# A two-layer streaming trunk: the first modulation entry by halves out of PSUM, and one gate vector worked out in the first FFN instead of the mixer

## The chip, the cores and the metric

The kernel runs on one core of a Trainium2 chip. The metric is the device time of one execution in microseconds (us). The time before is the median of three runs, 1248.64 us (1246.87 to 1248.95). All numbers below come from these runs and from one execution that the hardware profiler recorded.

## The reference

The model has two layers over 512 frames of width 1024, in fp32: one with an HGRN2 mixer and a SwiGLU FFN, then a K/V projection that reads its result, then one with band attention over that K/V and a second FFN. Every norm is followed by a shift and a scale, and every sublayer is added to the residual through a gate; shifts, scales and gates are rows of one product of silu(c) with `mod_w`. Cut to what matters here:

```python
c_act = jax.nn.silu(c)
for layer in range(2):
    mod = c_act @ mod_w[layer] + mod_b[layer]          # 1024 x 6144
    sh1, sc1, g1, sh2, sc2, g2 = jnp.split(mod, 6, axis=-1)
    u = modulate(rms_norm(h, norm_mix[layer]), sh1, sc1)   # u * (1 + scale) + shift
    mix = hgrn2_mixer(u, ...) if layer == 0 else chunk_band_attention(u, k, v, ...)
    h = h + g1[:, None, :] * mix
    u = modulate(rms_norm(h, norm_ffn[layer]), sh2, sc2)
    gate, up = jnp.split(u @ ffn_w_in[layer], 2, axis=-1)
    h = h + g2[:, None, :] * ((jax.nn.silu(gate) * up) @ ffn_w_out[layer])
    if layer == 0:
        k, v = shared_kv(h, c_act, ...)                # its own shift and scale
return rms_norm(h, final_norm)

# at the end of hgrn2_mixer, per head:
o = o * lax.rsqrt(jnp.mean(o * o, axis=-1, keepdims=True) + eps) * o_gain
o = o * silu(g)
return o.reshape(...) @ w_out
```

## The kernel before

**Layout.** Activations lie transposed: 8 blocks of 128 channels on the partitions, 512 frames along the free axis. A matrix product in fp32 is made as three passes of rounded parts, high x high, low x high, high x low (`mm3`, L184 to L186 in the profile). ScalarE makes each high part (names with `_h`; L120, L517), VectorE each low part (`_l`; L127, L518). The second and larger part of each FFN's input runs as "fast" tiles with seven products in place of eight: their weights `w1` to `w4` are combined on VectorE from the loaded blocks `c1` and `c2` (`f_x`, L531 to L536), then split, and their matmuls carry L552 to L554. The first FFN's tile 0 is made during the norm, tiles 1 to 3 are plain, and the rest are fast.

**Modulation vectors.** A vector has eight entries of 128 channels, one column each. For an entry a row of `mod_w` transposed, 128 x 1024, is loaded from HBM, and VectorE multiplies it with `crow`, silu(c) copied to all partitions, and sums along the free axis into one column (L334). The names are `mw{i}_{j}`: vector i, entry j; 4 is `sh2`, 5 is `g2`, 13 is `sck`. A generator, `mod_vectors`, called `side`, makes one entry at each `next(side)`. It loads two entries ahead, on SyncE's queue, into four buffers. `state["mods_after"]` names the instruction behind which a scheduler may put such an entry. In the mixer `side` is drawn from between pieces of filler work (`push`), and in the last head pair at the steps that `LAST` lists. `drain(side)` ahead of the stage `ao` (the mixer's output product) draws what is left. In the first FFN the next `side` is drawn from between fast tiles.

**The start.** Everything up to the first projections is in program order (`manual_schedule`). TensorE makes silu(c) on all partitions into two PSUM banks (`pcs`, tiles `crow0` and `crow1`). `KEEP` fill-up matmuls follow on TensorE (L978). ScalarE copies three quarters to `crow`, VectorE one quarter (L979 to L981). Then `mod_entry(0, 1)` makes the scale of the first block: product L634, column `a` on ScalarE (L637). `rounded` makes the high part of the first block (L656), `rest` the low part (L659), `high` and `low` those of the first weights (`first_h` L644, `first_l` L647), and the first matmuls follow (L683). The loads of rows, of `h` and of the first weights alternate on SyncE's queue.

**End of the mixer.** The last head pair runs `core(3)`: product `o`, squares summed on ScalarE (`osq`, L849), their scaling on VectorE (`oms`, L852), the power on GpSimd (`ors`, L854), the product with `o` on VectorE (`oe`, L860), transposes on TensorE (`ot`, L869), the gate (`yq`, L889), and the stage `ao`. What the scheduler has put ahead of an instruction on its engine's queue runs first. The rest of the order is chosen at build time by that scheduler, and is the same in every run.

Of the kernel before, what the change touches and what calls it, by code (L numbers as in the profile page):

```python
# [9 lines left out]
F32 = mybir.dt.float32  # L10
F32R = mybir.dt.float32r
U8 = mybir.dt.uint8
AF = mybir.ActivationFunctionType
ALU = mybir.AluOpType

P = 128
D = 1024
S = 512
KT = D // P
# [15 lines left out]
C_NM = C_KVB + 16  # L35
# [17 lines left out]
V1_AFTER, CREDIT, RATES = 1, 3.0, (3.5, 16, 2.0, 56, 1.5)  # L53


KEEP = 5


EARLY = (3, 5)
# [6 lines left out]
def trunk(ctx: ExitStack, tc: tile.TileContext, d, out):  # L66
    nc = tc.nc
    T, A, V, G = nc.tensor, nc.scalar, nc.vector, nc.gpsimd
# [3 lines left out]
    sm = ctx.enter_context(tc.tile_pool(name="sm", bufs=3))  # L72
# [6 lines left out]
    cols = cst.tile([P, NCOL], F32, tag="cols", name="cols")  # L79
# [56 lines left out]
    state = {"loaded": 0, "split": 0, "used": 0}  # L136
# [262 lines left out]
    def ffn(layer, z0, u, g2, side, finish):  # L399
        nm = f"f{layer}"  # L400
        fast = layer in FAST
        with tc.tile_pool(name=nm, bufs=1) as fp:
            a = []
            raw_a = {}
            FIRST = FT - 16
            if fast:
                his, los, sums = fast_inputs(fp, *u, nm)

                def slot(j, s):
                    return his[j][:, s, :], los[j][s // 2][:, s % 2, :]  # L410

                u = [(his[k // 2][:, 2 * (k % 2):2 * (k % 2) + 2, :].rearrange("p a c -> p (a c)"),
                      los[k // 2][k % 2].rearrange("p a c -> p (a c)")) for k in range(KT)]

            def activated(n):

                if not fast or n == FT - 1:
                    return sm.tile([P, S], F32, tag="sq", name=f"{nm}_at{n}", bufs=2)

                g, e = divmod(n, 2) if n < FIRST else divmod(n - FIRST, 4)  # L420
                if e == 0:
                    tag, m = (f"ab{g}", 2) if n < FIRST else (f"xs{g}", 4)
                    raw_a[n] = fp.tile([P, m, S], F32, tag=tag, name=f"{nm}_ar{n}")
                return raw_a[n - e][:, e, :]

            def kept(n, at):
                a.append(at if fast else usplit(fp, f"a{n}", at, f"{nm}_a{n}"))

            for n in range(PLAIN if fast else FT):
                sg = sm.tile([P, S], F32, tag="ut", name=f"{nm}_s{n}", bufs=2)  # L430
                at = activated(n)
                if n == 0:
                    (tg, bg), (tu, bu) = z0
                    A.activation(sg, tg, AF.Silu, bias=bg)
                    V.scalar_tensor_tensor(at, tu, bu, sg, op0=ALU.add, op1=ALU.mult)
                else:
                    res = []
                    drain(proj((nm, n, 0), u, res))
                    if not fast:
                        next(side, None)  # L440
                        next(side, None)
                    elif n in (2, 3):
                        sums(1, n == 3)
                    drain(proj((nm, n, 1), u, res))
                    if not fast:
                        next(side, None)
                    A.activation(sg, res[0], AF.Silu)
                    V.tensor_mul(at, res[1], sg)
                kept(n, at)
                if fast and n in (1, 2):  # L450
                    sums(0, n == 2)
            if fast:
                fast_tiles(fp, nm, slot, activated, kept, side)


            room = [("sp0", 1), ("sp1", 1)] + [(f"uo{j}", 2) for j in range(4)] + [("x1", 1), ("x2", 1)]
            room += [(f"ab{g}", 1) for g in range(FIRST // 2)] + [(f"xs{g}", 2) for g in range(4)]
            places = []

            def parts(k):  # L460
                if isinstance(a[k], tuple):
                    return a[k]
                if not places:
                    tag, m = room.pop(0)
                    t = fp.tile([P, 2 * m, S], F32R, tag=tag, name=f"{nm}_p{k}")
                    places.extend((t[:, 2 * i, :], t[:, 2 * i + 1, :]) for i in range(m))
                ah, al = places.pop(0)
                A.activation(ah, a[k], AF.Copy)
                V.tensor_sub(al, a[k], ah)  # L469
                a[k] = ah, al  # L470
                return a[k]

            chunks = ((0, 8), (8, 8), (16, 6))
            if fast:

                pss = [bank(f"{nm}_o{n}_0") for n in range(2)]
                for ci, (k0, nk) in enumerate(chunks):
                    ws = [weight((nm, "o", n, ci)) for n in range(2)]
                    for kt in range(nk):
                        k = k0 + kt  # L480
                        if k + 1 < FT:
                            parts(k), parts(k + 1)
                        for w, ps in zip(ws, pss):
                            mm3(ps, w, kt, a[k], k == 0, k == FT - 1)
                    for _ in range(2):
                        next(side, None)
                for n, ps in enumerate(pss):
                    residual(n, ps, g2)
                    later = finish(n, slice(0, S))
            for n in range(2 if fast else 0, KT):  # L490
                ws = []
                cuts = (slice(0, S),) if n < KT - 1 or not layer else (slice(0, CUT), slice(CUT, S))
                for c in cuts:
                    ps = bank(f"{nm}_o{n}_{c.start}")
                    for ci, (k0, nk) in enumerate(chunks):
                        if c.start == 0:
                            ws.append(weight((nm, "o", n, ci)))
                        for kt in range(nk):
                            k = k0 + kt
                            if c.start and k in later:  # L500
                                later.pop(k)()
                            mm3(ps[:, c], ws[ci], kt, [x[:, c] for x in a[k]], k == 0, k == FT - 1)
                        for _ in range(1 + (fast and ci == 0)):
                            next(side, None)
                    residual(n, ps, g2, c)
                    later = finish(n, c)
            drain(side)
# [96 lines left out]
    crow = mp.tile([P, D], F32, tag="crow", name="crow", bufs=1)  # L604
    mix = ctx.enter_context(ExitStack())
    hp = mix.enter_context(tc.tile_pool(name="hgrn", bufs=1))
# [5 lines left out]
    fraw, mrow, wfs, u, sqs, a1 = {}, {}, {}, {}, {}, []  # L612
# [18 lines left out]
    def mod_entry(j, v):  # L631
        raw = sm.tile([P, 1], F32, tag=f"m{v}", name=f"m{v}_{j}", bufs=4)
        mw = mrow.pop((j, v))
        V.scalar_tensor_tensor(mw, mw, 1.0, crow, op0=ALU.mult, op1=ALU.mult, accum_out=raw)  # L634
        r = sm.tile([P, 1], F32, tag=f"a{v}", name=f"a{v}_{j}", bufs=KT)
        if v:
            A.activation(r, raw, AF.Identity, scale=cols[:, C_NM + j:C_NM + j + 1], bias=gb[:, j:j + 1])  # L637
        else:
            A.activation(r, raw, AF.Identity, bias=cols[:, C_MB + j:C_MB + j + 1])
        return r  # L640

    def high(j):
        wfs[j] = [wp.tile([P, 6, P], F32R, tag="w" + x, name=f"first{j}_{x}") for x in "hl"]
        A.activation(wfs[j][0], fraw[j], AF.Copy)  # L644
# [41 lines left out]
    mod = {v: cst.tile([P, KT], F32, tag=f"mod_{v}", name=f"mod_{v}") for v in vectors[2:]}  # L686
# [251 lines left out]
            yield from output_gate(hd)  # L938

    late = []  # L940
    side = mod_vectors(("g1", "sc2", "sh2", "g2"), hp)
    MODS_FROM = 84
    fill = filler()
    pos = 0
# [13 lines left out]
    with tc.manual_schedule():  # L958
        dcs = hp.tile([P, KT, P], F32, tag="on3", name="dc")

        pcs = []
# [13 lines left out]
        gb = cst.tile([P, KT], F32, tag="gb", name="gb")  # L975
        V.scalar_tensor_tensor(gb, cols[:, C_MB + 8:C_MB + 16], 1.0, cols[:, C_NM:C_NM + KT], op0=ALU.add, op1=ALU.mult)
        for _ in range(KEEP):
            T.matmul(first[0][:, 0:256], ones, dcs[:, 0:2, :].rearrange("p k c -> p (k c)"), start=True, stop=True)  # L978
        A.activation(crow[:, 0:S], pcs[0], AF.Copy)  # L979
        A.activation(crow[:, S:S + 256], pcs[1][:, 0:256], AF.Copy)  # L980
        V.tensor_copy(crow[:, S + 256:D], pcs[1][:, 256:S])  # L981
        high(0)
        a1.append(mod_entry(0, 1))
        rounded(0)
        square(0)
        for j in range(KT):
# [98 lines left out]
        u = [u[j] for j in range(KT)]  # L1085
# [8 lines left out]
    on = [ons[i // 2][:, i % 2, :] for i in range(AH)]  # L1094
    ad = hp.tile([P, 2, NB, P], F32, tag="ad", name="ad")
    G.memset(ad, 0.0)
    LAST = {8: 3, 9: 1, 11: 1}
    for p in range(4):
        start, end = pos, ends[p]
        for i, _ in enumerate(core(p, *gate[p])):  # L1100
# [23 lines left out]
    for n in range(KT):  # L1124
# [4 lines left out]
        else:  # L1129
            res = []  # L1130
# [5 lines left out]
    z0, rb = early_pair((("f0", 0, 0), ("f0", 0, 1)), us, acc, "n1")  # L1136
# [3 lines left out]
    if 0 in FAST:  # L1140
        u = rb, a_f, mod["sh2"]
# [12 lines left out]

    shifts[("k", 0)] = shifts[("k", 1)] = mod["shk"]
    with tc.tile_pool(name="mx", bufs=1) as mx:
        ffn(0, z0, u, mod["g2"], mod_vectors(("sck", "shk", "sc1b", "sh1b", "g1b"), mx), finish)


    a_q = gain_scale(C_NM + KT, mod["sc1b"], "a_q")  # L1160
# [2 lines left out]
    with tc.tile_pool(name="attn", bufs=1) as ap:  # L1163
# [169 lines left out]
        for n in range(KT):  # L1333
# [4 lines left out]
            else:  # L1338
                res = []
# [215 lines left out]
```

## Time and profile before

| what | before |
|---|---|
| median of the runs | 1248.64 us (1246.87 to 1248.95) |
| the profiled execution | 1251.22 us |
| its span, first to last instruction | 1249.3 us |
| TensorE busy | 1230.0 us, 98% of the span |
| VectorE busy | 991.8 us, 79% |
| ScalarE busy | 648.1 us, 52% |
| GpSimd busy | 21.4 us, 2% |
| read from HBM | 171.96 MB |
| products of modulation rows, L334 | 96 in 115.6 us, 1219 ns each |

How to read the rows that follow. In the order of time a row is: start in us, length in us, engine, line, operation, output from inputs, shape and count, and in brackets the idle time ahead of it with the engine that ended it. In the chain of work that ended last a row is: start, length, what. In a view by stretches a row is: the stretch, busy us of the engines in the order TensorE, its weight loads, VectorE, ScalarE, GpSimd (with the count of instructions), the granted clock of TensorE as a share of full speed, the busy share of the DMA engines and GB/s; a row for TensorE alone leaves the other engines out. In a view of loads, "us from issue to landing" stands below the group's row.

### The profile page before, as it was taken

What the parts mean: (1) busy time and instruction counts of PE and PEld (TensorE: products, weight loads), DVE (VectorE), ACT (ScalarE), POOL (GpSimd) and SP (SyncE); (2) the same over time, 40 slices, a digit from 0 to 9 for tenths busy, and PEclk for the clock granted to TensorE, in tenths of its full rate; (3) what the DMA queues carried; (4) which work ended last, traced back from release to release, by engine and by line L of the source; (5) the groups of instructions that cost most, each with busy time, mean ns of one, the idle gap of its engine ahead of it and who ended that gap; (6) DMA issues with size and microseconds to landing.
All of it is one profiled execution on the core that took longest, in us unless ns stands there. A gap on an engine that the chain in (4) does not pass through costs nothing.

```text
span 1249.3 us, 21601 instructions
## 1 busy us (share of the span) xinstructions
PE 1230.0 (98%) x8548; PEld 1067.5 (85%) x8548; DVE 991.8 (79%) x1800; ACT 648.1 (52%) x1157; POOL 21.4 (2%) x29
## 2 busy tenths in 40 slices
PE   8999999999999999999999999999999999999997
PEld 7887778778899999988888877777889999998887
DVE  8986868877989999987668878996798999984323
ACT  6455446433655565642228556675455555573221
POOL 0100000000000000000000000000000000000000
PEclk9999999999999999999999999999999999999999
DMA  9632444543424444467752445531243444342331
GB/s 364 239 130 86 136 153 155 194 159 118 107 96 137 150 142 146 139 205 274 240 177 77 135 134 163 163 109 65 71 122 113 138 136 135 102 127 93 93 93 68
DMA packets 52533, 177.55 MB, mean 142 GB/s; under 512 B 5968, under 2 KB 8400, under 8 KB 52432
## 3 DMA queue, kind: packets, MB, share of 16 engines
q1 hardware_dynamic: 51856, 174.08, 42.4%
q0 software_dynamic: 576, 2.10, 1.0%
q8 instruction: 67, 1.10, 0.4%
q14 instruction: 34, 0.28, 0.1%
HBM read 171.96 MB, written 2.10 MB: 139 GB/s over the span
## 4 chain that ended last, share of the span: by engine, by line
PE 87%; DVE 6%; ACT 3%; issue 1%; DMA 1%; POOL 0%; DVEq 0%; POOLq 0%; ACTq 0%
PE f_r L553 10%; PE f_r L554 9%; PE f_r L552 9%; PE f_o L185 6%; PE f_o L186 6%; PE f_o L184 6%; PE f L184 2%; PE f L185 2%; PE f L186 2%; PE bo L1258 1%; PE bo L184 1%; PE ao L184 1%; PE ao L185 1%; PE ao L186 1%; PE bo L186 1%
## 5 line engine op out<-in xcount | busy, mean ns | idle before, releaser
L553 PE MATMUL f_r<-f_l,f_w_h 128*128 128x256 f32 x1008 | 287.8, 285 | 0.0
L554 PE MATMUL f_r<-f_h,f_w_l 128*128 128x256 f32 x1008 | 282.2, 280 | 0.0
L552 PE MATMUL f_r<-f_h,f_w_h 128*128 128x256 f32 x1008 | 281.2, 279 | 0.0
L552 PEld LDWEIGHTS f_r<-f_h,f_w_h 128*128 128x128 f32 x1008 | 190.1, 189 | 0.1
L553 PEld LDWEIGHTS f_r<-f_l,f_w_h 128*128 128x128 f32 x1008 | 190.0, 189 | 0.1
L554 PEld LDWEIGHTS f_r<-f_h,f_w_l 128*128 128x128 f32 x1008 | 189.3, 188 | 0.0
L185 PE MATMUL f_o<-f_p,f_o_h 128*128 128x512 f32 (+1 forms) x374 | 141.9, 379 | 0.1
L184 PE MATMUL f_o<-f_p,f_o_h 128*128 128x512 f32 (+1 forms) x374 | 141.8, 380 | 0.0
L186 PE MATMUL f_o<-f_p,f_o_l 128*128 128x512 f32 (+1 forms) x374 | 141.4, 379 | 0.0
L334 DVE SCALAR_TENSOR_TENSOR mw<-mw,crow 128x1024 f32<-128x1024 f32 x96 | 115.6, 1219 | 2.3 <-DMA mw<-in_modw 2.3
L120 ACT ACTIVATE f_o_h<-r_f_o 128x1024 fp32r<-128x1024 f32 (+1 forms) x48 | 46.8, 987 | 133.5 <-PE f_o L185 102.6
L127 DVE TENSOR_TENSOR f_o_l<-r_f_o,f_o_h 128x1024 fp32r<-128x1024 f32 (+1 forms) x48 | 54.1, 1133 | 69.3 <-ACT f_o_h L120 61.6
L517 ACT ACTIVATE f_w_h<-f_x 128x1024 fp32r<-128x1024 f32 x72 | 76.5, 1062 | 51.1 <-PE f_r L553 43.8
L518 DVE TENSOR_TENSOR f_w_l<-f_x,f_w_h 128x1024 fp32r<-128x1024 f32 x72 | 88.1, 1225 | 9.3 <-ACT f_w_h L517 4.6
L517 ACT ACTIVATE f_w_h<-r_f_c 128x1024 fp32r<-128x1024 f32 x72 | 61.0, 847 | 50.6 <-PE f_r L553 48.2
L186 PEld LDWEIGHTS f_o<-f_p,f_o_l 128*128 128x128 f32 x374 | 70.2, 188 | 14.9 <-DVE f_o_l L127 1.3
L185 PEld LDWEIGHTS f_o<-f_p,f_o_h 128*128 128x128 f32 x374 | 70.4, 188 | 13.5 <-DVE f_p L469 0.5
L184 PEld LDWEIGHTS f_o<-f_p,f_o_h 128*128 128x128 f32 x374 | 70.4, 188 | 13.3
L518 DVE TENSOR_TENSOR f_w_l<-r_f_c,f_w_h 128x1024 fp32r<-128x1024 f32 x72 | 68.7, 954 | 9.0 <-ACT f_w_h L517 9.0
L1233 ACT ACTIVATE sb<-sb,st 128x128 f32<-128x128 f32 (+1 forms) x64 | 35.8, 560 | 30.3 <-DVE st L1232 29.8
L185 PE MATMUL f<-f_l,f_h 128*128 128x512 f32 x96 | 37.4, 396 | 0.0
L186 PE MATMUL f<-f_h,f_l 128*128 128x512 f32 x96 | 37.1, 393 | 0.0
(402 smaller groups left out, 2718.7 us busy)
## 6 DMA issues: line engine op xcount, KB each, us to landing
mw<-in_modw SPq DMA_DIRECT2D x96, 512.0 KB, 4.3
r_f_c<-in_ffn_in SPq DMA_DIRECT2D x72, 512.0 KB, 3.4
r_f_o<-in_ffn_out SPq DMA_DIRECT2D x32, 512.0 KB, 3.7
mrow<-in_modw SPq DMA_DIRECT2D x16, 512.0 KB, 7.9
r_f<-in_ffn_in SPq DMA_DIRECT2D x16, 512.0 KB, 3.4
r_f_o<-in_ffn_out SPq DMA_DIRECT2D x16, 384.0 KB, 3.4
r_av<-in_a_v SPq DMA_DIRECT2D x8, 512.0 KB, 4.5
r_g<-in_a_g SPq DMA_DIRECT2D x8, 512.0 KB, 3.4
```

The costliest lines, as they stand in the source:

```text
L120: A.activation(wh, raw, AF.Copy)
L127: low = V.tensor_sub(wl, raw, wh)
L184: T.matmul(ps, wh[:, kt, :], uh, start=start, stop=False)
L185: T.matmul(ps, wh[:, kt, :], ul, start=False, stop=False)
L186: T.matmul(ps, wl[:, kt, :], uh, start=False, stop=stop)
L334: V.scalar_tensor_tensor(mw, mw, 1.0, crow, op0=ALU.mult, op1=ALU.mult, accum_out=raw[:, j:j + 1])
L517: A.activation(wh, raw, AF.Copy)
L518: V.tensor_sub(wl, raw, wh)
L552: T.matmul(ps, wh[:, j, :], uh, start=f, stop=False, skip_group_check=True)
L553: T.matmul(ps, wh[:, j, :], ul, start=False, stop=False, skip_group_check=True)
L554: T.matmul(ps, wl[:, j, :], uh, start=False, stop=stop and j == 3, skip_group_check=True)
L1233: A.activation(s[:, 0:n], s[:, 0:n], AF.Exp, bias=st[:, 1:2], accum_out=st[:, 2:3])
```

## The change

It has two parts.

At the start, the first entry is made in two halves of 512. Each reads its half of silu(c) directly from the PSUM bank, as soon as the bank is full (L988). Two small ScalarE instructions (L990) chain the halves: the first adds its sum to `gb`, the second adds its own to that. ScalarE then copies the first half of `crow` (L995) and VectorE the second (L993), for the later entries. The fill-up matmuls go from five calls to three.

The vector `g2` is taken out of the mixer's `side` (24 entries instead of 32) and put first in that of the first FFN (48 instead of 40). In that FFN two entries are drawn behind each of the plain tiles 1, 2 and 3, placed after the tile's product. `LAST` becomes `{8: 2}`.

```diff
-KEEP = 5
+KEEP = 3
...
-                    V.tensor_mul(at, res[1], sg)
+                    state["mods_after"] = V.tensor_mul(at, res[1], sg)
                 kept(n, at)
+                if fast and not layer and n:
+                    for _ in range(2):
+                        next(side, None)
...
-        r = sm.tile([P, 1], F32, tag=f"a{v}", name=f"a{v}_{j}", bufs=KT)
+        r = sm.tile([P, 1], F32, tag=f"a{v}", name=f"a{v}_{j}", bufs=KT + 1)
...
-    side = mod_vectors(("g1", "sc2", "sh2", "g2"), hp)
+    side = mod_vectors(("g1", "sc2", "sh2"), hp)
...
-        A.activation(crow[:, 0:S], pcs[0], AF.Copy)
-        A.activation(crow[:, S:S + 256], pcs[1][:, 0:256], AF.Copy)
-        V.tensor_copy(crow[:, S + 256:D], pcs[1][:, 256:S])
-        high(0)
-        a1.append(mod_entry(0, 1))
+        m2 = [sm.tile([P, 1], F32, tag="m1", name=f"m1_0{r}", bufs=4) for r in range(2)]
+        mw = mrow.pop((0, 1))
+        a = gb[:, 0:1]
+        for r in range(2):
+            half = slice(r * S, (r + 1) * S)
+            V.scalar_tensor_tensor(mw[:, half], mw[:, half], 1.0, pcs[r], op0=ALU.mult, op1=ALU.mult, accum_out=m2[r])
+            t = sm.tile([P, 1], F32, tag="a1", name=f"a1_0{r}", bufs=KT + 1)
+            A.activation(t, m2[r], AF.Identity, scale=cols[:, C_NM:C_NM + 1], bias=a)
+            a = t
+            if r:
+                V.tensor_copy(crow[:, half], pcs[r])
+            else:
+                A.activation(crow[:, half], pcs[r], AF.Copy)
+                high(0)
+        a1.append(a)
         rounded(0)
...
-    LAST = {8: 3, 9: 1, 11: 1}
+    LAST = {8: 2}
...
-        ffn(0, z0, u, mod["g2"], mod_vectors(("sck", "shk", "sc1b", "sh1b", "g1b"), mx), finish)
+        ffn(0, z0, u, mod["g2"], mod_vectors(("g2", "sck", "shk", "sc1b", "sh1b", "g1b"), mx), finish)
```

The order of the instructions on VectorE is what the second part moves. In the rows below a name carries a running number at its end, and the lines of the changed kernel lie three further down.

VectorE at the start, before: the copy of a quarter of `crow`, the whole first product, the low parts of the first weights and of the first block, and the next product.

```order
L981 COPY crow_106<-crow1_141 128x256
L634 SCALAR_TENSOR_TENSOR mrow1_0_150,m1_0_215<-mrow1_0_150,crow_106 128x1024
L647 TENSOR_TENSOR first0_l_213<-first_r0_153,first0_h_212 128x768
L659 SCALAR_TENSOR_TENSOR u00l0_220<-h0_71,a1_0_217,u00h0_219 128x512
L634 SCALAR_TENSOR_TENSOR mrow1_1_155,m1_1_225<-mrow1_1_155,crow_106 128x1024
```

The same place after.

```order
L988 SCALAR_TENSOR_TENSOR mrow1_0_150,m1_00_207<-mrow1_0_150,crow0_132 128x512
L988 SCALAR_TENSOR_TENSOR mrow1_0_150,m1_01_208<-mrow1_0_150,crow1_141 128x512
L993 COPY crow_106<-crow1_141 128x512
L650 TENSOR_TENSOR first0_l_214<-first_r0_153,first0_h_213 128x768
L662 SCALAR_TENSOR_TENSOR u00l0_221<-h0_71,a1_01_217,u00h0_220 128x512
L637 SCALAR_TENSOR_TENSOR mrow1_1_155,m1_1_226<-mrow1_1_155,crow_106 128x1024
```

Two half-products that read the PSUM tiles now stand ahead of a copy that is twice as large; the rest keeps its order.

VectorE at the end of the mixer, before: entries of `sh2` and `g2`, the gates `yq` of head 4, the low part of an `ao` weight, then the norm of the last head pair (`oms3`, `oe6`).

```order
L334 SCALAR_TENSOR_TENSOR mw4_7_2799,mcol4_2429<-mw4_7_2799,crow_106 128x1024
L334 SCALAR_TENSOR_TENSOR mw5_1_2805,mcol5_2863<-mw5_1_2805,crow_106 128x1024
L337 TENSOR_TENSOR mod_sh2_119<-mcol4_2429,cols_67 128x8
L334 SCALAR_TENSOR_TENSOR mw5_0_2802,mcol5_2863<-mw5_0_2802,crow_106 128x1024
L889 TENSOR_TENSOR yq4_2895<-on2_879,yq4_2895 128x512
L334 SCALAR_TENSOR_TENSOR mw5_2_2861,mcol5_2863<-mw5_2_2861,crow_106 128x1024
L889 TENSOR_TENSOR yq4_2895<-on2_879,yq4_2895 128x512
L127 TENSOR_TENSOR ao_1_l_2903<-r_ao_1_2783,ao_1_h_2902 128x1024
L365 TENSOR_TENSOR f0_sh1_3376<-mod_sh2_119 128x4
L852 TENSOR_SCALAR oms3_2848<-oss3_2809 128x8
L860 TENSOR_TENSOR oe6_2868<-o6_2810,ors3_2850 128x512
```

After:

```order
L334 SCALAR_TENSOR_TENSOR mw4_7_2800,mcol4_2430<-mw4_7_2800,crow_106 128x1024
L892 TENSOR_TENSOR yq4_2882<-on2_880,yq4_2882 128x512
L337 TENSOR_TENSOR mod_sh2_119<-mcol4_2430,cols_67 128x8
L892 TENSOR_TENSOR yq4_2882<-on2_880,yq4_2882 128x512
L127 TENSOR_TENSOR ao_1_l_2890<-r_ao_1_2784,ao_1_h_2889 128x1024
L365 TENSOR_TENSOR f0_sh1_3351<-mod_sh2_119 128x4
L855 TENSOR_SCALAR oms3_2843<-oss3_2804 128x8
L863 TENSOR_TENSOR oe6_2858<-o6_2805,ors3_2845 128x512
```

The three entries of `g2` are gone from ahead of `oms3`; the other instructions stand as they stood.

VectorE in the input stage of the first FFN, around the preparation of fast tiles 4 and 5 (`f0_ar2` is the product of plain tile 3), before:

```order
L536 TENSOR_TENSOR f0_4_x2_3643<-r_f0_4_c1_3570,f0_4_x1_3642 128x512
L518 TENSOR_TENSOR f0_4_w2_l_3651<-f0_4_x1_3642,f0_4_w2_h_3650 128x1024
L531 TENSOR_TENSOR f0_5_x1_3721<-r_f0_5_c2_3640,r_f0_5_c1_3638 128x512
L448 TENSOR_TENSOR f0_ar2_3482<-f0_3_1_3605,f0_s3_3569 128x512
L518 TENSOR_TENSOR f0_4_w3_l_3657<-f0_4_x2_3643,f0_4_w3_h_3656 128x1024
```

After:

```order
L539 TENSOR_TENSOR f0_4_x2_3638<-r_f0_4_c1_3559,f0_4_x1_3637 128x512
L521 TENSOR_TENSOR f0_4_w2_l_3646<-f0_4_x1_3637,f0_4_w2_h_3645 128x1024
L448 TENSOR_TENSOR f0_ar2_3465<-f0_3_1_3594,f0_s3_3558 128x512
L334 SCALAR_TENSOR_TENSOR mw5_3_3546,mcol5_3452<-mw5_3_3546,crow_106 128x1024
L334 SCALAR_TENSOR_TENSOR mw5_4_3549,mcol5_3452<-mw5_4_3549,crow_106 128x1024
L521 TENSOR_TENSOR f0_4_w3_l_3652<-f0_4_x2_3638,f0_4_w3_h_3651 128x1024
```

Two entries of `g2` stand between the product of tile 3 and the low part of the third weight pair of tile 4. Of the other entries, `mw5_0` stands behind the product of tile 1, `mw5_1` and `mw5_2` behind that of tile 2, and `mw5_5` and the later ones come among the fast tiles, where entries of `sck` stood. On TensorE the order is the same but for the fill-up matmuls.

## The prediction

> **What bounds the kernel now.** I read the page first, then the stretches, then the chain of waits at the places that the change touches, then the engines in order of time there.
>
> ```profile
> PE 87%; DVE 6%; ACT 3%; issue 1%; DMA 1%; POOL 0%; DVEq 0%; POOLq 0%; ACTq 0%
> ```
>
> TensorE carries 87% of the chain that ended last, and the change leaves its order as it was but for two fill-up matmuls. So only places where TensorE waits, or runs at a lower clock, can give time back, and only new waits can cost any. Two stretches (busy us of PE, PEld, DVE, ACT, POOL, then granted clock, DMA share and GB/s):
>
> ```profile
> 240.00:260.00 20.00, 17.48 (x94) 15.25 (x95) 15.57 (x27) 8.48 (x26) 1.64 (x1) 0.91 0.72 234
> ...
> 320.00:340.00 20.00, 20.00 (x88) 16.27 (x87) 19.14 (x34) 15.96 (x26) 1.91 (x2) 1.00 0.46 108
> ```
>
> The first, the end of the mixer, is the one with idle TensorE (2.5 us of 20) and a clock of 0.91. The second, the input stage of the first FFN, has a full TensorE and a VectorE busy for 19.14 of 20 us: that is where the change puts work. The chain of waits through the first (start, length, what):
>
> ```profile
> 239.91 2.00 DVE mw L334 x3
> ...
> 242.23 6.41 DMA mw<-in_modw
> ...
> 248.67 1.23 DVE mw L334 x2
> ...
> 251.94 1.65 POOL ors L854
> ```
>
> A row of the gate vector g2 (`mw5_2`) could be loaded only when the buffer of an earlier row was free, took 6.41 us to land, and stood on VectorE's queue ahead of `oms` (L852), which starts the norm of the last head pair. The same place in order of time:
>
> ```profile
> 249.57 0.22 ACT L849 ACTIVATION_READ_ACCUMULATOR osq<-o 128x1 f32 x1
> ```
> ```profile
> 251.63 0.16 DVE L852 TENSOR_SCALAR oms<-oss 128x8 f32<-128x8 f32 x1
> ```
> ```profile
> 251.60 0.39 PE L186 MATMUL g<-u0h,g_l 128*128 128x512 f32 x1
> 254.45 1.94 PE L869 MATMUL ot<-ident,oe 128*128 128x128 f32 x8 [2.46 <-DVE oe L860]
> ...
> 257.88 0.40 PE L185 MATMUL ao<-yq,ao_h 128*128 128x512 f32 x1
> ```
>
> The data of `oms` was complete at 249.79, `oms` ran at 251.63, and TensorE stood for 2.46 us until the transposes at 254.45.
>
> **End of the mixer: the g2 rows go.** In the new order no g2 row stands ahead of `oms`. VectorE's last row there, `mw4_7`, is followed by two `yq`, `mod_sh2`, one `ao_l` and a tiny add. Today `mw4_7` and the first `yq` are these:
>
> ```profile
> 242.12 1.22 DVE L334 SCALAR_TENSOR_TENSOR mw<-mw,crow 128x1024 f32<-128x1024 f32 x1
> ...
> 245.63 0.69 DVE L889 TENSOR_TENSOR yq<-on,yq 128x512 fp32r<-128x512 f32 x1
> ```
>
> With 0.69 for each `yq` and at most 1.23 for `ao_l`, VectorE is free near 243.3 + 3.0 = 246.3, some 3 us before 249.79. `oms` then waits for ScalarE alone and starts at about 249.85: 1.78 us earlier. What follows it (1.65 on GpSimd, `oe`, handovers) is the 2.82 us from 251.63 to 254.45 and stays. So the transposes start at 252.67, and 0.68 us of the gap remains. First term: **-1.8**; below by no more than the gap (2.46), and towards 0 only if VectorE were late by another route, for which 3 us of slack leave no room.
>
> The gap has a second price, the clock (PE busy, granted clock, DMA share, GB/s):
>
> ```profile
> 254.00:255.00 1.00, 0.55 (x3) 0.71 0.76 307
> 255.00:256.00 1.00, 1.00 (x7) 0.50 0.00 0
> ...
> 257.00:258.00 1.00, 1.00 (x4) 0.58 0.96 246
> ```
> ```profile
> 240.00:241.00 1.00, 0.94 (x5) 1.00 0.96 369
> ```
> ```profile
> 240.06 1.96 PE L826 MATMUL l<-qq,ks 128*128 128x256 f32 x8 [1.48 <-DVE ks L749]
> ```
> ```profile
> 127.14 1.04 PE L869 MATMUL ot<-ident,oe 128*128 128x128 f32 x8
> ...
> 128.96 0.39 PE L185 MATMUL zf<-u0l,zf_h 128*128 128x512 f32 x1
> ```
>
> A mean of 0.71 over 254 to 255 puts the fall to one half at about 254.42, 2.4 us into the gap; 0.58 over 257 to 258 puts its return at 257.84. Behind a gap of 1.48 us the clock stayed at 1.00. An earlier head pair had the same eight transposes with no gap ahead: from the first of them to the fifth large matmul behind, 127.14 to 128.96, 1.82 us; here 254.45 to 257.88, 3.43 us. The half clock cost 1.61 us. With 0.68 us of gap, less than half of the one that did no harm, I take the whole: **-1.6**, between 0 (the fall comes anyway) and -1.7 (half of the 3.42 us).
>
> The Trainium skill, page "TensorE: Matmul & The Clock Gate", section "Why this matters for your kernels", asks for no gap above about 3 us, and "What's actually happening" there has the gate judge by free-running windows of about 3.4 us. This trace differs on the length: 2.46 us of idling were followed by half clock. By that rule alone the loss would not be this gap's, and the sum would be without its 1.6.
>
> No queue pays for the move here: on SyncE's queue the `ao` weights from `r_ao_4` on have two g2 loads ahead of them instead of seven, and GpSimd's order is unchanged. What is late next is ScalarE's `osq`, which sets `oms`.
>
> **Start.** The chain there, and the rows beside it:
>
> ```profile
> 7.38 0.39 ACT crow L980
> ...
> 7.79 0.44 DVE crow L981
> ...
> 9.52 0.40 ACT a L637
> ...
> 9.94 0.73 ACT u00h L656
> ...
> 10.71 4.38 PE first L683 x18
> ...
> 15.55 0.50 PE first L186
> ```
> ```profile
> 7.82 0.84 ACT L644 ACTIVATE first_h<-first_r 128x768 fp32r<-128x768 f32 x1
> ```
> ```profile
> 8.25 1.23 DVE L634 SCALAR_TENSOR_TENSOR mrow<-mrow,crow 128x1024 f32<-128x1024 f32 x1
> ...
> 12.51 1.22 DVE L634 SCALAR_TENSOR_TENSOR mrow<-mrow,crow 128x1024 f32<-128x1024 f32 x1
> ...
> 14.54 0.96 DVE L647 TENSOR_TENSOR first_l<-first_r,first_h 128x768 fp32r<-128x768 f32 x1
> ```
> ```profile
> 7.13 3.09 PE L978 MATMUL first<-dc,ones 128*128 128x256 f32 x10
> ```
> ```profile
> L624 SPq DMA_DIRECT2D mrow<-in_modw x1: 557/557/557, 4.6 to 4.6; - x1
> ...
> DMA to landing us min/median/max: 7.4/7.4/7.4
> ```
> ```profile
> 266.95 0.75 DVE L350 SCALAR_TENSOR_TENSOR h<-ao,mod_g,h 128x512 f32<-128x512 f32 x1 [2.00 <-PE ao L186]
> ```
>
> The two copies and the 1.23 us product go off the path; the second half-product can start when the second bank is full, at 7.38. No row shows such a half with an accumulator out of PSUM. Its bounds are half of 1.23, 0.6, and the residual at 266.95, which reads PSUM at this size: 0.75. I take 0.75 and 0.1 for the accumulator: done near 8.25. But ScalarE gets to the second `a` only behind `first_h`, 8.66, so this price decides nothing. From `a` to TensorE it is 1.19 us now (9.52 to 10.71): TensorE starts at about 9.85, 0.85 earlier. The fill-up work is 0.31 us a matmul record, 6 for 10, and ends near 9.0: it holds nothing up.
>
> Not all of it arrives. The next thing TensorE waits for is `first_l` of the second block, at 15.55, behind two products and a rest on VectorE. The first `rest`, at the earliest 9.9, moves the product behind it up by as much as itself, but the one after that, now at 12.51, needs the third row, which lands at 4.6 + 7.4 = 12.0: 0.5 earlier. Then `first_l` runs at about 13.9, 0.6 earlier, since it also follows ScalarE. After 15.55 TensorE goes without a wait. Second place: **-0.6**, from 0 (the rows land later than here) to -0.85.
>
> **Input stage of the first FFN.** Five rows of g2 come in there, behind the tiles 1, 2 and 3, at 1.22 us each: 6.1 us of VectorE; three more fall into the fast tiles, where before another vector's rows stood, and all later vectors move back by eight rows. What has least room is the low part of the third weight pair of tile 4, which now stands behind `mw5_3` and `mw5_4`:
>
> ```profile
> 349.63 0.69 DVE L531 TENSOR_TENSOR f_x<-r_f_c,r_f_c 128x512 f32<-128x512 f32 x1 [2.27 <-DMA r_f_c<-in_ffn_in]
> ...
> 350.85 1.22 DVE L518 TENSOR_TENSOR f_w_l<-f_x,f_w_h 128x1024 fp32r<-128x1024 f32 x1
> ```
> ```profile
> 348.35 0.28 PE L552 MATMUL f_r<-f_h,f_w_h 128*128 128x256 f32 x1
> ...
> 354.06 0.28 PE L552 MATMUL f_r<-f_h,f_w_h 128*128 128x256 f32 x1
> ```
> ```profile
> 646.53 1.23 DVE L127 TENSOR_TENSOR k_l<-r_k,k_h 128x1024 fp32r<-128x1024 f32 x1 [2.71 <-ACT k_h L120]
> ```
>
> Today that low part is done at 352.0, and TensorE uses it in a later product of the tile, from 354.06: 2.1 us of room. In the new order these two rows start when tile 3 is complete, about 348.6, in a stretch where VectorE now waits 2.27 us for a weight; the two take 2.4, and with 0.3 for handovers the low part ends near 352.7. The three rows before them delay the products that wait for another weight anyway. Cost **0**; if the cover is gone, up to 6.1. The loads: `r_f0_5_c2` stands behind two rows on SyncE's queue, but needs a buffer that is free later than theirs. At the end of this FFN one row more is drained, 1.2 us, ahead of `k_l`, where VectorE has 2.71 us to spare: 0.
>
> **Sum.** -1.8 - 1.6 - 0.6 = -4.0 us. On the profiled execution: 1251.22 to 1247.2 (its span 1249.3 to 1245.3). The median of the runs is 2.6 below that execution, so the forecast is 1248.64 - 4.0 = 1244.6 us. A change within 0.2% (2.5 us) is about what a measurement of this kernel can't tell from none.
>
> **Rivals.** (a) The clock loss isn't in the timed runs. The fall came 0.03 us ahead of the transposes: a moment later it would have missed part of them, and one of the three runs, 1246.87, is 1.8 below the others. Then the gain is 1.8 + 0.6 = 2.4, to 1246.2. The skill's rule on windows, above, would have it so in some runs. Against it: the two other runs agree within 0.3 us. Chance 0.2. (b) VectorE is full in the FFN's input stage, 19.14 of 20 us, and half of the five rows shows up at TensorE, 3 us of small waits: the gain shrinks to 1.0, to 1247.6. Against it: the 2.1 us of room and the waits on loads. 0.1. (c) Slower: the rows delay the low part at 350.85 by more than 4.5 us, so that TensorE waits over 2.4 us at 354.06 and the clock falls there too: all 6.1 on the path less 2.1 of room, and 1.6 for the clock, 5.6 against 4.0 won: 1250.2, and over 1251 if later tiles follow. It decides from 2.4 us of wait on. 0.05. (d) The start gives nothing, since the rows land later: 3.4 won, 1245.2. 0.1. The forecast has 0.55.
>
> From these: faster by over 0.2% 0.72 (the forecast, (d), and a third of (a)), same 0.23, slower 0.05. Range 1243.0 to 1247.4: at the low end all three terms at their bounds, 0.85 + 2.1 + 1.7 = 4.65, and 1.0 for the scatter of a median whose runs lie 2 apart; at the high end (a) with 1.2 of scatter or of small waits. It leaves out (c) and a part of (b).
>
> **What would show it.** After the change: `oms` directly behind the last `osq`; a gap of about 0.7 us before `ot`, eight transposes in about 1.0 instead of 1.94 and a clock of 1.00 in that stretch; the first large matmul at about 9.9 and the wait before `first_l` of the second block kept; no new wait on TensorE between 330 and 365. Wrong if the transposes still run at half clock, if TensorE waits for `f_w_l` of tile 4 or 5, or if the second block starts where it does now.

## The result, and the profile after

The changed kernel takes 1257.67 us (median of 4 runs, 1256.08 to 1258.53), the kernel before in the same comparison 1247.96 us (4 runs, 1246.87 to 1248.95). The ratio is 1.0077, with a 95% interval of 1.0059 to 1.0094: slower by 9.7 us, where 4.0 us less were forecast. The profiled execution of the changed kernel spans 1256.6 us.

The chain of waits, by engine, has less of TensorE and more of the transfers than before:

```profile
PE 85%; DVE 7%; ACT 3%; issue 2%; DMA 2%; SPq 0%; POOL 0%; DVEq 0%; POOLq 0%; ACTq 0%
```

The two stretches of the prediction, in the same columns (TensorE, weight loads, VectorE, ScalarE, GpSimd, granted clock, DMA share, GB/s):

```profile
240.00:260.00 20.00, 19.32 (x108) 16.47 (x109) 10.99 (x19) 8.46 (x26) 1.64 (x1) 1.00 0.33 106
320.00:340.00 20.00, 17.51 (x71) 13.88 (x70) 19.37 (x35) 14.02 (x23) 1.91 (x2) 0.92 0.51 131
```

At the end of the mixer TensorE is busy for 19.32 of the 20 us now, at full clock, as forecast. The FFN's input stage has taken over both of its losses: 2.5 us without TensorE, and a clock of 0.92. TensorE's waits between 200 and 420 name the new one (waited for, total, times, longest):

```profile
PE f L186 <- DMA f_l<-r_f: 2.5, 1, 2.5
...
PE ot L872 <- DVE oe L863: 0.7, 1, 0.7
```

A third loss has no wait at all. These are TensorE's busy time, count of instructions, clock, DMA share and GB/s in a stretch of fast tiles and one of output products, before:

```profile
400.00:500.00 100.00, 100.00 (x843) 1.00 0.44 143
560.00:640.00 80.00, 80.00 (x351) 1.00 0.73 241
```

and after:

```profile
400.00:500.00 100.00, 100.00 (x835) 1.00 0.44 139
560.00:640.00 80.00, 80.00 (x346) 1.00 0.72 239
```

TensorE is never idle in either, and the clock is 1.00 in both, but it gets through 835 matmuls where it got through 843, and through 346 for 351. Matched one by one, the same instructions fall behind by 0.19 us in every 20 us of fast tiles and by 0.30 us in every 20 us of output products, in both FFNs; the projections of the mixer and most of the attention keep their pace. Over some 370 us of fast tiles and 210 us of output products that is 3.5 + 3.2 = 6.7 us.

### The profile page after: what moved, and what is told of

The parts are those of the page before. It is cut to its first block, busy times and chain, and to the rows that moved or that the text cites. A ratio compares the mean times of both kernels' runs of the same rounds, so it can differ in the third digit from the quotient of the medians.

```text
span 1256.6 us, 21596 instructions
## 1 busy us (share of the span) xinstructions
PE 1236.3 (98%) x8544; PEld 1069.4 (85%) x8544; DVE 991.5 (79%) x1802; ACT 648.4 (52%) x1157; POOL 21.4 (2%) x29
## 4 chain that ended last, share of the span: by engine, by line
PE 85%; DVE 7%; ACT 3%; issue 2%; DMA 2%; SPq 0%; POOL 0%; DVEq 0%; POOLq 0%; ACTq 0%
PE f_r L555 10%; PE f_r L557 10%; PE f_r L556 9%; PE f_o L185 6%; PE f_o L186 6%; PE f_o L184 6%; PE o L849 1%; PE bo L1272 1%; PE f L186 1%; PE bo L184 1%; PE f L184 1%; PE ao L186 1%; PE ao L185 1%; PE ao L184 1%; PE bo L186 1%
## 5 line engine op out<-in xcount | busy, mean ns | idle before, releaser
L555 PE MATMUL f_r<-f_h,f_w_h 128*128 128x256 f32 x1008 | 286.7, 284 | 0.0
L557 PE MATMUL f_r<-f_h,f_w_l 128*128 128x256 f32 x1008 | 286.2, 284 | 0.0
L556 PE MATMUL f_r<-f_l,f_w_h 128*128 128x256 f32 x1008 | 283.2, 281 | 0.0
L184 PE MATMUL f<-f_h,f_h 128*128 128x512 f32 x96 | 37.5, 401 | 0.0
```

Source lines behind the costliest of these rows:

```text
L184: T.matmul(ps, wh[:, kt, :], uh, start=start, stop=False)
L555: T.matmul(ps, wh[:, j, :], uh, start=f, stop=False, skip_group_check=True)
L556: T.matmul(ps, wh[:, j, :], ul, start=False, stop=False, skip_group_check=True)
L557: T.matmul(ps, wl[:, j, :], uh, start=False, stop=stop and j == 3, skip_group_check=True)
```

## The experiments

Two theories and their rivals came from this. Theory P: one more buffer for each of the columns `a0` and `a1` (`KT + 1` in the diff) puts every tile that is allocated behind them 64 bytes per partition higher, the FFNs' activations among them, and TensorE reads those more slowly. Rival D: the moved loads, or something else of that execution. Theory T: the load of a g2 row shares the DMA engines with the transfer that makes tile 3's low weight part. Rival V: VectorE's added work delays it.

**Place alone, and the change without it.** `before_up64` moves the tiles in the kernel before and nothing else:

```diff
-        r = sm.tile([P, 1], F32, tag=f"a{v}", name=f"a{v}_{j}", bufs=KT)
+        r = sm.tile([P, 1], F32, tag=f"a{v}", name=f"a{v}_{j}", bufs=KT + 1)
```

> The kernel before with one more buffer for each of the two tags of the columns a0 and a1 that nothing uses: the order of every engine stays, and every tile behind those small tiles (both FFNs' activations among them) lies 64 bytes per partition higher, as in the changed kernel. Theory P (placement): the matmuls of both FFNs get slower as in the changed kernel, by 0.19 us in 20 in the fast tiles and 0.30 in 20 in the output products, together 6.6 us over 1248, so about 1254.6. Rival D (the moved loads or the chip made TensorE slower): no change, 1248.0.

Measured: 1254.49 us (1254.08 to 1254.83), ratio 1.0054 (95% interval 1.0042 to 1.0067; further down such an interval stands in square brackets). The rates are those of the changed kernel:

```profile
400.00:500.00 100.00, 100.00 (x835) 1.00 0.44 142
560.00:640.00 80.00, 80.00 (x346) 1.00 0.74 242
```

`after_at0` is the changed kernel with all engines' orders unchanged and the tiles back at their old places:

```diff
-        raw = sm.tile([P, 1], F32, tag=f"m{v}", name=f"m{v}_{j}", bufs=4)
+        raw = sm.tile([P, 1], F32, tag=f"m{v}", name=f"m{v}_{j}", bufs=3 + v)
...
-        r = sm.tile([P, 1], F32, tag=f"a{v}", name=f"a{v}_{j}", bufs=KT + 1)
+        r = sm.tile([P, 1], F32, tag=f"a{v}", name=f"a{v}_{j}", bufs=KT + v)
```

> The changed kernel with the same instructions in the same order, but one buffer less for a0 and for m0, so that all tiles behind lie where they lay in the kernel before. Theory P: 6.6 us less than the changed kernel, about 1251: 3.3 won at the end of the mixer and 4.2 lost in the FFN's input stage remain. Rival D: stays at 1257.7.

Measured: 1249.08 us (1248.01 to 1250.63), ratio 1.0015 [1.0006, 1.0024], with the rates of the kernel before:

```profile
400.00:500.00 100.00, 100.00 (x843) 1.00 0.43 143
560.00:640.00 80.00, 80.00 (x351) 1.00 0.75 247
```

Theory P holds: the 64 bytes cost 6.7 us (5.2 to 8.4) without the rest of the change, and 8.6 us (1257.67 against 1249.08, in two comparisons) are gone when they are taken back. The 1249.08 is 2 us below what was expected: six of its runs lie between 1248.0 and 1249.1 and five between 1249.8 and 1250.6, the profiled one, with wait and half clock, among the upper. The mean granted clock on record for each run parts the two groups: 0.997 in each of the five, 0.998 or 0.999 in the six. Of the profiles here, the four with half clock behind a wait have 0.997 or 0.998, the ten without it 0.998 or 0.999. So the lower six most likely keep the full clock, though they were not profiled, and that would explain most of the 1.9 us by which 8.6 exceeds 6.7.

**The wait on f_l.** The order at the place in the changed kernel's chain (start, length, what):

```profile
329.26 7.44 DMA f_l<-r_f
336.70 0.04 issue
336.74 0.79 PE f L186
```

`f_l` is the low weight part of plain tile 3. It is not made on VectorE, as the other low parts are: ScalarE writes minus the high part, and a transfer that GpSimd issues adds the raw weight on top. TensorE ran dry at 334.2, 5.0 us behind the issue. Before, the issue and the first matmul that reads its result were these, 4.9 us apart:

```profile
332.81 1.05 POOL L125 DMA_DIRECT2D f_l<-r_f  x1 [24.61 <-DVE f_s L383]
```
```profile
337.73 0.39 PE L186 MATMUL f<-f_h,f_l 128*128 128x512 f32 x1
```

The two such transfers took 4.7 and 5.5 us from issue to landing there, the first of them the shorter, so the room was 0.2 to 0.3 us. On SyncE's queue in the changed kernel stands, 0.5 us ahead of that issue:

```profile
328.79 0.33 SPq L323 DMA_DIRECT2D mw<-in_modw  x1
```

This is the load of `mw5_4`, into the buffer that `mw5_0` behind tile 1 has just left free. `after_rows_late` takes the draws away behind tile 1 and makes them up behind tile 2, so that VectorE has the same rows to do in the stage, and the load comes later:

```diff
-                if fast and not layer and n:
-                    for _ in range(2):
+                if fast and not layer and n > 1:
+                    for _ in range((4, 2)[n - 2]):
                         next(side, None)
```

> The changed kernel, but none of the g2 rows behind plain tile 1: three behind tile 2, two behind tile 3. VectorE does the same work in the stage, but no row's load starts while the first transfer of tile 3's low weight part runs. Theory T (the row loaded from 328.8 shares the DMA engines with that transfer): the wait of 2.5 us and the half clock behind it go, 4.2 less, about 1253.5, with no wait on f_l. Rival V (VectorE's work in the stage): the wait stays or turns up a tile later, 1256 to 1258.

Measured: 1254.1 us (1253.73 to 1255.11), ratio 1.0053 [1.0039, 1.0066], with no wait on `f_l`, and the two transfers back at their old times (issue to landing, min, median, max):

```profile
DMA to landing us min/median/max: 4.7/5.1/5.5
```

`row1_kept` is the opposite, at the old places: the row behind tile 1 and its load stay, and VectorE has a row less behind tile 2.

```diff
-                    for _ in range(2):
+                    for _ in range((2, 1, 2)[n - 1]):
```

> The changed kernel at the old places, with one g2 row behind tile 1 as there, but one instead of two behind tile 2: VectorE has 1.2 us less to do in the stage, while the load of mw5_4 still follows the row behind tile 1, into the first transfer of tile 3's low weight part. Theory T (the load): the wait of 2.2 to 2.5 us and the half clock stay, the transfer takes about 7.2 us again and not 5.5. Theory V (VectorE's work): the wait shrinks to about 1 us or less, and no half clock.

Measured: 1250.45 us (one run; the kernel before beside it 1248.53). The wait is whole, and the transfers are slow:

```profile
PE f L186 <- DMA f_l<-r_f: 2.4, 1, 2.4
```
```profile
DMA to landing us min/median/max: 6.4/6.9/7.4
```

One row less on VectorE behind tile 2 changes nothing, and without the load at that moment the wait is gone: Theory T. In both runs the row behind tile 1 goes or stays together with its load, and the row that `row1_kept` leaves out comes only after the transfer's issue, so they alone don't free the row behind tile 1. The changed kernel's trace does:

```profile
327.54 1.22 DVE L334 SCALAR_TENSOR_TENSOR mw<-mw,crow 128x1024 f32<-128x1024 f32 x1
```

That row is over at 328.76, half a microsecond ahead of the issue at 329.26, and the issue stands as far ahead of its use as before. What grew is the transfer itself, from 4.7 to 7.4 us. That the two share the DMA engines is the likely reason; shown is that they run at the same time. The clock paid as well, as it had before at the end of the mixer (TensorE in the changed kernel):

```profile
336.00:337.00 1.00, 0.26 (x1) 0.89 0.83 160
337.00:338.00 1.00, 1.00 (x3) 0.50 0.29 57
...
340.00:341.00 1.00, 1.00 (x6) 0.90 0.65 168
```

Half clock from about 336.8 to 340.2, one stretch of 3.4 us, so 1.7 us lost behind a wait of 2.5: 4.2 us.

**Both mended, and what is left of the gain.** `after_at0_rows_late` has both edits.

> Both edits, placement of the kernel before and no g2 row behind tile 1. Theories P and T: the 3.3 us won at the end of the mixer are all that is left, 1248.0 - 3.3 = 1244.7. If either is wrong, 1249 to 1253.

Measured: 1246.36 us (1245.61 to 1247.03), ratio 0.9989 [0.998, 0.9998]. Both losses are gone, but 0.8 us came out where 3.3 were expected. So the kernel before was profiled once more.

> The kernel before, unchanged, profiled in another execution. Theory S (the stall at the end of the mixer was one execution's: a load of 6.4 us that mostly lands earlier): the wait of TensorE ahead of the transposes is 0.7 us and not 2.5, no half clock, and the execution takes about 3.3 us less than the one of 1251.22. Rival, as the prediction had it (the stall is in every execution): 2.5 us of wait and half clock again.

Measured: 1247.23 us. In this execution of the same kernel the gap ahead of the transposes is small, and the row that stood in the way, the one behind the first `yq`, lands in time:

```profile
252.96 1.16 PE L869 MATMUL ot<-ident,oe 128*128 128x128 f32 x8 [0.66 <-DVE oe L860]
```
```profile
247.06 1.23 DVE L334 SCALAR_TENSOR_TENSOR mw<-mw,crow 128x1024 f32<-128x1024 f32 x1 [0.42 <-DMA mw<-in_modw]
```

VectorE waits 0.42 us for it, and not 2.34; eight transposes take 1.16 us at full clock. TensorE runs 3.4 us earlier from there on than in the execution that the prediction was read from, and that is what it had meant to win. The other five profiles of orders with the g2 rows in the mixer have gaps of 0.7 us (four) and 1.7 us (`before_up128`). Of the 44 runs of the kernel before in the two largest comparisons (21 and 23 runs) five lie above 1249, between 1249.76 and 1250.73, each with a mean granted clock of 0.997; the other 39 lie between 1245.99 and 1248.66, with 0.998 or 0.999. So about one execution in nine most likely had the stall with its half clock. It is not shown, since none of the five was profiled.

**The parts alone**, at the old places. `start_only_at0` has the halves and the three fill-up calls, with the second part undone; `g2_only_at0_rows_late` has g2 in the first FFN, drawn as in `after_rows_late`, with the first part undone.

> The kernel before with the first part of the change alone (first entry by halves, three fill-up calls), with every tile behind the small ones at its old place (one buffer less for m0 pays for the one more for a1). From the profiles so far (the second block at 23.62 of the kernel before comes 0.0, 0.0, 0.6 and 1.2 us earlier, by how soon the first weights and the third row land): 0.5 us on average, 1246.7 against 1247.2, not to be told from no change. If the start carries all of what the last comparison showed: 0.8 less, 1246.4. The prediction's term was 0.6.

Measured: 1246.45 us (1245.68 to 1246.88), ratio 0.999 [0.9981, 0.9998].

> The kernel before with the second part alone, g2 in the first FFN with no row behind plain tile 1, every tile at its old place. Theory S (the stall at the end of the mixer is in few executions): 1246.5 to 1247.2, no more than 0.7 less, and fewer executions of 1249 and above. The prediction's view (the stall is in all): 3.3 less, 1243.9.

Measured: 1246.88 us (1246.27 to 1247.28), ratio 0.9993 [0.9984, 1.0001]. The second part is worth nothing that can be told from no change in most executions; none of its 11 runs is above 1247.3. The first part's 0.8 us may be real, but its profile has TensorE's first blocks only 0.1 us earlier, so where it would come from stays open.

**Other places.** If 64 bytes cost 0.5%, others might win. Three kernels are the one before with the tiles higher by 32, 128 and 192 bytes:

```diff
-        r = sm.tile([P, 1], F32, tag=f"a{v}", name=f"a{v}_{j}", bufs=KT)
+        r = sm.tile([P, 1], F32, tag=f"a{v}", name=f"a{v}_{j}", bufs=KT + v)    # 32; KT + 2: 128; KT + 3: 192
```

> The kernel before with those tiles 32 bytes higher. If the cost grows with the distance from the old place: about half of that of 64 bytes, 3.5 us, 1250.7. If 64-byte lines count, a tile that starts inside one costs as much as at 64 bytes or more: 1254 or above. If the old place is only one of several good ones: 1247 or below.

> The kernel before with the tiles behind the small ones 128 bytes per partition higher. If the cost has a period of 128 bytes: no change of rate in either FFN (0.0 in 20 us) and 1247. If every place but the old one costs: 0.2 to 0.3 in 20 us and 1254.

> The kernel before with those tiles 192 bytes higher. Period of 128 bytes: the same cost as 64 bytes, 1254.5. Otherwise a rate of its own, possibly below that of the kernel before: its best matmuls of 256 columns follow one another in 116.4 ns, its mean is 118.9, so up to 2% of the FFNs' time could still be won by place.

Measured, one run each: 1251.44, 1249.95 and 1246.22 us, beside 1249.52 of the kernel before on that chip. The rates, in this order, 32 first:

```profile
400.00:500.00 100.00, 100.00 (x846) 1.00 0.44 145
560.00:640.00 80.00, 80.00 (x345) 1.00 0.72 236
```
```profile
400.00:500.00 100.00, 100.00 (x851) 1.00 0.43 145
560.00:640.00 80.00, 80.00 (x344) 1.00 0.72 237
```
```profile
400.00:500.00 100.00, 100.00 (x836) 1.00 0.43 141
560.00:640.00 80.00, 80.00 (x354) 1.00 0.72 239
```

Neither the distance from the old place nor a period of 128 bytes fits. The two kinds of matmul want different places: the fast tiles (256 columns, `f_h` moved, `f_l` and the weights not) run best at 128, the output products (512 columns, `f_p` moved) at 192. `best_place` gives each its own, in the kernel with both parts and the late rows: everything 192 higher, `f_h` another 192 within tiles that are 256 bytes longer.

```diff
-        his = [fp.tile([P, 8, H], F32R, tag=f"uo{j}", name=f"{nm}_h{j}") for j in range(KT // 2)]
+        his = [fp.tile([P, 8 * H + 64], F32R, tag=f"uo{j}", name=f"{nm}_h{j}")[:, 48:48 + 8 * H].rearrange("p (a c) -> p a c", c=H)
+               for j in range(KT // 2)]
...
-                    t = fp.tile([P, 2 * m, S], F32R, tag=tag, name=f"{nm}_p{k}")
+                    t = fp.tile([P, 2 * m * S + 64 * tag.startswith("uo")], F32R, tag=tag, name=f"{nm}_p{k}")
+                    t = t[:, 0:2 * m * S].rearrange("p (a c) -> p a c", c=S)
```

> The kernel with both parts and no g2 row behind tile 1, with places chosen from the shifts: all tiles behind the small ones 192 bytes higher, and the first parts of the FFNs' input (f_h) 192 bytes further on in tiles that are 256 bytes longer, so 128 bytes higher by 256. If the cost has a period of 256 bytes and the shifts add up by operand: 0.19 less in 20 us of fast tiles, 0.20 less in 20 us of output products, 0.5 each in the mixer's output stage and in attention, together about 6.5 less than the same kernel at the old places (1246.4): 1239.9. If the period is longer: between 1240 and 1250, with different rates for the four f_h tiles.

Measured: 1241.27 us (1240.81 to 1241.62), ratio 0.9946 [0.9934, 0.9958], the fastest version here. Both stretches have the better rate:

```profile
400.00:500.00 100.00, 100.00 (x851) 1.00 0.43 144
560.00:640.00 80.00, 80.00 (x355) 1.00 0.75 248
```

The four `f_h` tiles lie 8448 bytes apart, which is 33 times 256, and run alike, so a period of 256 bytes fits. The 5.1 us against the same kernel at the old places (1246.36, in another comparison) are less than the 6.5 expected. Matched one by one, the matmuls from 260 to 340 us gain 0.2 us, where `before_up192` had gained 1.0, and those from 860 to 940 us gain nothing, where it had gained 0.7.

## Why the prediction was wrong, point by point

- **Terms -1.8 and -1.6 (end of the mixer).** The mechanism was right, and the changed kernel shows it done: `oms` directly behind ScalarE, at 249.71 for the 249.85 forecast, a gap of 0.68, eight transposes in 1.16 us at full clock.

```profile
249.71 0.17 DVE L855 TENSOR_SCALAR oms<-oss 128x8 f32<-128x8 f32 x1 [4.00 <-ACT osq L852]
```
```profile
252.54 1.16 PE L872 MATMUL ot<-ident,oe 128*128 128x128 f32 x8 [0.68 <-DVE oe L863]
```

  The step that failed is the last one of the sum: 3.4 us that were read from an execution of 1251.22 us were taken off a median of 1248.64. The 2.6 us between the two were noted and not asked about. Most executions don't have the stall: against the one of 1247.23 us the same change wins about 0.4 us there (the transposes at 252.54 for 252.96). Rival (a) came near, but had only the clock missing from most runs, and not the wait.

- **Input stage, cost 0.** The search for room in this stage went through VectorE's queue and one load on SyncE's (`r_f0_5_c2`), and left out the transfers that GpSimd issues. VectorE's place of least room, the low part of tile 4's third weights, held; no wait on `f_w_l` appeared. What had the least room was the first of these transfers, 0.2 to 0.3 us, and the price of a load beside it was 2.7 us (7.4 for 4.7 us). Rival (c) had this stage, a wait over 2.4 us and half clock behind it, with the wrong resource and a chance of 0.05. Its price, 5.6, was 4.2.

- **The diff's `KT + 1`** was given no term at all, and it is the largest: 6.7 us. The step that failed is the one that all terms rest on, "only new waits can cost any". It takes TensorE's pace as given where its order is unchanged. The runs show 835 matmuls for 843, and 346 for 351, with the same order, no wait and a clock of 1.00.

- **Start, -0.6.** Rival (d) is what the changed kernel's execution shows: the rows and weights land later than the halves are ready.

```profile
8.71 0.84 ACT L647 ACTIVATE first_h<-first_r 128x768 fp32r<-128x768 f32 x1 [1.31 <-DMA first_r<-in_a_first]
...
10.64 1.66 PE L686 MATMUL first<-u00h,first_h 128*128 128x512 f32 x6 [1.00 <-ACT u00h L659]
```

  ScalarE was ready 1.31 us before the first weights, and TensorE starts at 10.64, not at 9.85. In the profiles with the new start `first_h` begins between 7.78 and 8.71, by when that load lands, and TensorE between 9.98 and 10.64; with the old start TensorE began between 10.55 and 10.79. The term's own 0.6 went by the third row, expected at 12.0. In the changed kernel it landed at 12.86, and TensorE got to the second block's `first_l` at 15.71, where the kernel before had been at 15.55:

```profile
4.54 8.32 DMA mrow<-in_modw
...
15.71 0.50 PE first L186
```

  For TensorE's start, the step that failed is the 8.66 behind which ScalarE "gets to the second `a`": it took `first_h` as it ran before, while `first_h` itself now waits, for a load that the old chain hid.

- **The range.** Its low end says that all three terms stand at their bounds, but takes 2.1 for the first, whose bound was the whole gap, 2.46. With that the low end would have been 1242.6. It decides nothing here: the time lies above the high end.

- **The clock.** In the profiles, gaps of 2.46, 2.5, 2.2 (`after_at0`) and 2.4 us (`row1_kept`) were all followed by half clock, for 3.4 us each time, and one of 1.67 us (`before_up128`) and those of 1.5 were not. In these four traces the fall lies a whole number of stretches of 3.413 us behind the first record of the clock, 72 in the kernel before and 96 in the other three. So where a gap falls most likely counts beside its length, which fits the two groups of `after_at0`. The Trainium skill, page "TensorE: Matmul & The Clock Gate", section "Why this matters for your kernels", asks for no gap above about 3 us; the runs show the harm earlier. The length of the half-clock stretch agrees with the free-running window of about 3.4 us that its section "What's actually happening" gives.

The account of the 9.7 us: 6.7 for place, 2.7 to 3.6 for the wait on `f_l` and its clock (1249.08 - 1246.36, and 1257.67 - 1254.1, the latter from two comparisons), less the 0.8 that is left of the gain: 8.6 to 9.5.

## What to carry to other kernels

A stall in one profile is worth what it costs in the runs that are compared: where the profiled execution lies above the median by about the size of the stall, profile it again before counting it. An added buffer, however small, moves all tiles behind it; compare the rate of a stretch in which nothing waits before and after, and try a few offsets, since they can be worth more than the change. Before a load is moved into a stage, list the transfers that the stage itself makes, and how much room the first of them has.

## What was not expected of the hardware

TensorE's pace without any wait depends on where the activations that it reads as its moving operand lie in SBUF: the same 256-column matmuls came 835 to 851 in 100 us, and the same 512-column ones 344 to 355 in 80 us, at offsets of 0, 32, 64, 128 and 192 bytes, and the offsets rank differently for the two kinds. `best_place` moved `f_h` apart from the rest, and the rate of the fast tiles went with `f_h`. The place moves the cost between matmuls as well. By the start times in the traces, a matmul of `f_h` with `f_w_h` is followed by the next after 117.5 ns on average in the kernel before and 121.6 ns in `before_up64`. Behind one of `f_l`, which was not moved, it is 122.1 and 118.0 ns. Of the Trainium skill, page "SBUF — State Buffer", section "Specifications (TRN2)", the rule nearest to this is that SBUF has cachelines of 16 bytes; all offsets here are multiples of 32, so by that rule they should run alike, and they do not. Why is not settled: of the operands of these matmuls only the activations were moved, never the weights or the outputs.
